# Tying each transfer that sums feed-forward weights to one split of a piece of weights

## The chip, the cores and the metric

The kernel runs on one core of one Trainium2 chip. The metric is the device time of one execution, in microseconds (us): a median of 2010.33 us over three runs, which lay between 2003.17 and 2014.34 us. TensorE (PE) multiplies, VectorE (DVE) and ScalarE (ACT) do the work on elements, GpSimd (POOL) does little arithmetic here, SyncE (SP) only issues transfers. The transfers of all issuers run on the core's 16 DMA engines.

## The reference

Two blocks of a language model work on one sequence of 512 tokens with 1024 features, in float32. The first block projects its normed input on 4104 columns, runs a gated delta rule (4 heads) and a differential attention (4 heads), and projects back. The second block puts 16 tokens in front (528 tokens), and then has a feed-forward layer (`ffn1`), a mixer (retention, and an attention that picks 128 keys for each query), a second feed-forward layer (`ffn2`) and a norm. Its core, cut down:

```python
def swiglu(u, w_gate, w_up, w_down):                     # w_gate, w_up: 1024 x 2816
    return (jax.nn.silu(u @ w_gate) * (u @ w_up)) @ w_down

x = first_block(x, norm_gain, w_in, conv_w, ...)         # gated delta rule, differential attention
h = concatenate([meta, x])                               # 528 tokens
h = h + 0.5 * swiglu(rmsnorm_2(h, ffn1_norm), ffn1_w_gate, ffn1_w_up, ffn1_w_down)
h = h + hybrid_mixer(rmsnorm_2(h, mix_norm), ...)
h = h + 0.5 * swiglu(rmsnorm_2(h, ffn2_norm), ffn2_w_gate, ffn2_w_up, ffn2_w_down)
y = rmsnorm_2(h, final_norm)[:, 16:]
```

## The kernel before

**Stages.** The program runs `block1`, `ffn` for ffn1, `mixer` and `final` (which holds ffn2). Features lie on the 128 partitions, tokens along the rows. Every product is made of float32r parts: weights and activations are split in a high and a low part, and three matmuls (lines 302 to 304, or 1042) make one product.

**The stream of weights.** All weights pass through one list of jobs. `_dma` (line 184) issues a load on SP's queue, into one of two buffers `wraw` (up to 512 KB) or one of eight buffers `fraw` (256 KB, quarters of feed-forward weights). `_conv` (line 249) then splits a piece of at most four 128x128 tiles: ACT copies the high part (`_split`, line 237), DVE subtracts it for the low part (line 238). This is the split of a piece of weights; most jobs have two pieces, a quarter has one. `convert` runs up to five pieces (`CONVB`) ahead of the matmuls.

**The sums of weights.** A feed-forward layer computes the gate and the up projection of 19 of its 22 column tiles by a scheme with fewer products, which needs four sums of weight quarters for each tile. `sum_weights` (line 206) makes them in DRAM: 80 transfers on POOL's queue for each layer (line 227), plain copies and copies that add to what lies there (`accum_op`), into ten tiles `wsums` (named `wsffn...` in the profile). The ten tiles are worked off in groups of three: 24 transfers for each of three groups, and 8 for the last tile. `sum_weights` is a generator: `_conv` asks it for the next transfer at every second split in block1, at every third split in ffn1 and in the mixer (lines 261 and 262, `bgn`). So this sets where a transfer stands in the program. It does not set when it starts: a transfer waits only for earlier transfers on the same tile, and for its turn on POOL's queue. The feed-forward stage reads the sums back as `fraw` quarters; such a load waits for the transfers that it depends on.

**What else stands in block1.** The projections (line 909 and after) run on PE in program order. Beside them a chain of small steps works on the gated delta rule: gates, a row vector sent through DRAM and loaded to all partitions (`rd`, line 562: four loads of 1 MB into `slot`), for each of four heads the decay matrix (DVE line 579, a triangular select on POOL line 580, ACT line 582, DVE lines 591 to 602), an inverse (lines 616 to 700) whose blocks go through DRAM (`db`, line 610; `dx`, lines 624 and 626), and a scan. Another chain works on the differential attention, and sends a norm through DRAM once for each head (`rdfd`, line 785, `krow`, line 788, used on DVE at line 791 and then on PE at line 819). A scheduler sets the order on each engine from the program and its own estimate of times.

Of the kernel before, what the change touches and what calls it, by code (L numbers as in the profile page):

```python
# [12 lines left out]
AF = mybir.ActivationFunctionType  # L13
OP = mybir.AluOpType
AX = mybir.AxisListType

D = 1024
KB = 8
# [150 lines left out]
class Net:  # L169
# [36 lines left out]
    def sum_weights(self, n):  # L206


        nc, a = self.nc, self.a
        nf = 22 - PLAIN  # L210
        out = self.wsums[n] = [self.dram.tile([min(2, nf - i), 4, 128, 4, 128], F32, name=f"ws{n}{i}")
                               for i in range(0, nf, 2)]
        rows = lambda x: x.rearrange("n p k c -> p n k c")

        def src(i, x):
            f = PLAIN + 2 * i
            o = 4 if x in "GU" else 0
            return a[n + ("_gate" if x in "gG" else "_up")][f:f + out[i].shape[0], :, o:o + 4, :]

        steps = (((0, "u"), (2, "g")), ((0, "U"), (2, "u")), ((1, 0),), ((1, "g"),), ((3, 1),), ((3, "G"),))  # L220
        for i0 in range(0, len(out), 3):
            for j, step in enumerate(steps):
                for i in range(i0, min(i0 + 3, len(out))):
                    for d, x in step:
                        y = out[i][:, x] if isinstance(x, int) else src(i, x)
                        kw = {"accum_op": OP.add} if j in (1, 3, 5) else {}
                        nc.gpsimd.dma_start(rows(out[i][:, d]), rows(y), **kw)
                        yield

    def _split(self, j, x):  # L230

        n, ncol = x.shape[1:]
        if j < len(self.joblist) - self.kept:
            hi, lo = (self.wpool.tile([128, n, ncol], F32R, name=y, tag=y, bufs=self.CONVB) for y in ("whi", "wlo"))
        else:
            hi, lo = self.keep(n)
        self.nc.scalar.copy(hi, x)  # L237
        self.nc.vector.tensor_sub(lo, x, hi.bitcast(F32))  # L238
        return hi, lo

# [8 lines left out]
    def _conv(self):  # L249

        j, k = self.j_conv, self.k_conv
        raw = self.raws[j]
        nk = raw.shape[1]
        n = min(self.CK, nk - k)
        hi, lo = self._split(j, raw[:, k:k + n, :])
        his, los = self.convd.setdefault(j, ([], []))
        his += [hi[:, i, :] for i in range(n)]
        los += [lo[:, i, :] for i in range(n)]
        self.n_conv += 1
        self.k_conv += n  # L260
        if self.n_conv % self.bgn == 0:
            next(self.bg, None)
        if self.k_conv == nk:
            self.raws.pop(j)
            if self.joblist[j][0] == "f":
                self.f_done += 1
            else:
                self.p_done += 1
            self.j_conv, self.k_conv = j + 1, 0
            self.prefetch()  # L270
# [124 lines left out]
    def block1(self):  # L395
# [3 lines left out]
        with es:  # L399
# [8 lines left out]
            def params():  # L408
# [4 lines left out]
                V.tensor_mul(lamv[:, 0::2, :], lamv[:, 0::2, :], lamv[:, 1::2, :])  # L413
                V.reduce_sum(lam, lamv[:, 0::2, :], axis=AX.X)
                A.activation(lam, lam, AF.Exp)
# [1296 lines left out]
```

## Time and profile before

| | |
|---|---|
| median of three runs | 2010.33 us |
| profiled execution | 2014.84 us, its span 2013.0 us |
| PE busy | 1920.7 us (95% of the span) |
| DVE busy | 1284.2 us (64%) |
| ACT busy | 904.4 us (45%) |
| POOL busy | 153.6 us (8%) |
| moved by DMA | 281.36 MB |
| POOL's queue (q0) | 79.70 MB, 17.4% of the 16 engines' span |
| SP's queue (q1) | 198.60 MB, 30.6% |

The stages lie in the span about so: block1 from 0 to 452 us, ffn1 to 800 us (its two stretches of quarters at 482 to 563 and 628 to 739 us), the mixer to about 1640 us, then ffn2 and the end. In a table by stretches, PE's busy time against the length of the stretch tells where PE stood still; the granted clock tells in which of its two levels (1.0 is 2.4 GHz, 0.5 is 1.2 GHz) it ran; the DMA share is the busy share of the 16 engines. Line numbers in the rows are those of the kernel before. In the changed kernel the same lines stand one to three lines further down.

### The profile page before, as it was taken

How to read it: one execution, taken by the hardware profiler on the slowest of the kernel's cores; microseconds unless marked ns; L12 is line 12 of the kernel's file. 1: busy time of each engine (PE TensorE's matmuls, PEld its weight loads, DVE VectorE, ACT ScalarE, POOL GpSimd, SP SyncE). 2: the span in 40 equal slices, each digit the busy share in tenths (PEclk: the TensorE clock that was granted, in tenths of full speed). 3: DMA queues.
4: the chain of work that ended last, by engine and by line, in shares of the span. 5: the costliest groups of instructions: out<-in, count | busy, mean ns of one | idle time of the engine just before them, and what ended most of it. 6: DMA issues, size and time to landing. Idle time of an engine off the chain costs nothing.

```text
span 2013.0 us, 31731 instructions
## 1 busy us (share of the span) xinstructions
PE 1920.7 (95%) x12138; PEld 1705.7 (85%) x12138; DVE 1284.2 (64%) x2590; ACT 904.4 (45%) x1774; POOL 153.6 (8%) x179
## 2 busy tenths in 40 slices
PE   6957878999999999999999999999999999999998
PEld 3746657889999999888989898888888889989997
DVE  3645654766746765889755454687764467756764
ACT  3523444555634653445343434344443346634653
POOL 3322432320000000000000000000000000000000
PEclk8978878999999999999999999999999999999999
DMA  9999999994534533321222221211122234535532
GB/s 278 264 245 229 256 240 234 268 249 139 181 105 143 182 110 97 114 73 69 95 68 95 69 89 61 97 63 64 64 74 95 94 122 138 185 108 156 183 103 92
DMA packets 119607, 281.36 MB, mean 140 GB/s; under 512 B 16192, under 2 KB 18720, under 8 KB 119392
## 3 DMA queue, kind: packets, MB, share of 16 engines
q1 hardware_dynamic: 86816, 198.60, 30.6%
q0 software_dynamic: 31552, 79.70, 17.4%
q8 instruction: 95, 1.56, 0.3%
q10 hardware_dynamic: 1088, 1.05, 0.1%
q14 instruction: 56, 0.46, 0.1%
HBM read 276.63 MB, written 82.36 MB: 178 GB/s over the span
## 4 chain that ended last, share of the span: by engine, by line
PE 82%; DMA 12%; DVE 3%; issue 2%; POOL 0%; ACT 0%; SPq 0%; DVEq 0%; POOLq 0%; ACTq 0%
PE pm L302 18%; PE pm L304 18%; PE pm L303 18%; PE pm L1042 11%; DMA wsffn<-in_ffn_up 4%; PE so L1042 3%; PE sc L1042 3%; PE st L1042 3%; DMA wsffn<-wsffn 2%; DMA wsffn<-in_ffn_gate 2%; PE sc L302 2%; PE sc L303 1%; PE sc L304 1%; DMA krow<-rdfd 1%; DVE rot L1208 1%
## 5 line engine op out<-in xcount | busy, mean ns | idle before, releaser
L237 ACT CAST whi<-wraw 128x512 fp32r<-128x512 f32 (+1 forms) x476 | 276.9, 584 | 611.9 <-PE pm L303 462.1
L302 PE MATMUL pm<-xhi,whi 128*128 128x264 f32 (+3 forms) x1448 | 503.7, 348 | 12.0 <-DVE xc L909 10.9
L303 PE MATMUL pm<-xlo,whi 128*128 128x264 f32 (+3 forms) x1448 | 495.8, 342 | 0.0
L304 PE MATMUL pm<-xhi,wlo 128*128 128x264 f32 (+3 forms) x1448 | 494.5, 341 | 0.0
L238 DVE TENSOR_TENSOR wlo<-wraw,whi 128x512 fp32r<-128x512 f32 (+1 forms) x476 | 305.1, 641 | 220.5 <-ACT whi L237 211.3
L302 PEld LDWEIGHTS pm<-xhi,whi 128*128 128x128 f32 (+1 forms) x1448 | 276.4, 191 | 46.7 <-DVE xc L909 11.3
L304 PEld LDWEIGHTS pm<-xhi,wlo 128*128 128x128 f32 (+1 forms) x1448 | 276.1, 191 | 31.3 <-issue 2.7
L303 PEld LDWEIGHTS pm<-xlo,whi 128*128 128x128 f32 (+1 forms) x1448 | 276.4, 191 | 28.6 <-issue 2.0
L237 ACT CAST whi<-fraw 128x512 fp32r<-128x512 f32 x266 | 164.8, 619 | 155.0 <-PE pm L1042 30.3
L238 DVE TENSOR_TENSOR wlo<-fraw,whi 128x512 fp32r<-128x512 f32 x266 | 183.4, 690 | 72.0 <-ACT whi L237 53.7
L302 PE MATMUL pm<-ahi,whi 128*128 128x264 f32 (+1 forms) x506 | 160.1, 316 | 0.0
L304 PE MATMUL pm<-ahi,wlo 128*128 128x264 f32 (+1 forms) x506 | 159.9, 316 | 0.0
L303 PE MATMUL pm<-alo,whi 128*128 128x264 f32 (+1 forms) x506 | 159.3, 315 | 0.0
L1042 PE MATMUL pm<-thi,whi 128*128 128x264 f32 (+1 forms) x456 | 129.7, 284 | 0.0
L1042 PE MATMUL pm<-thi,wlo 128*128 128x264 f32 (+1 forms) x456 | 129.1, 283 | 0.0
L1042 PE MATMUL pm<-tlo,whi 128*128 128x264 f32 (+1 forms) x456 | 129.0, 283 | 0.0
L302 PEld LDWEIGHTS pm<-ahi,whi 128*128 128x128 f32 x506 | 95.2, 188 | 6.0
L303 PEld LDWEIGHTS pm<-alo,whi 128*128 128x128 f32 x506 | 95.2, 188 | 5.9
L304 PEld LDWEIGHTS pm<-ahi,wlo 128*128 128x128 f32 x506 | 95.1, 188 | 5.9
L1632 POOL TENSOR_TENSOR hg<-hg,rcol 128x256 f32<-128x256 f32 x4 | 2.8, 730 | 1198.8 <-ACT rcol L1627 1198.8
L1042 PEld LDWEIGHTS pm<-thi,whi 128*128 128x128 f32 x456 | 86.6, 190 | 0.9 <-DVE u L1082 0.9
L1042 PEld LDWEIGHTS pm<-tlo,whi 128*128 128x128 f32 x456 | 86.7, 190 | 0.0
(482 smaller groups left out, 3842.3 us busy)
## 6 DMA issues: line engine op xcount, KB each, us to landing
wraw<-in_w_in SPq DMA_DIRECT2D x124, 512.0 KB, 3.3
fraw<-wsffn SPq DMA_DIRECT2D x152, 256.0 KB, 2.7
wsffn<-in_ffn_up POOLq DMA_DIRECT2D x54, 512.0 KB, 15.7
wsffn<-in_ffn_gate POOLq DMA_DIRECT2D x54, 512.0 KB, 10.8
fraw<-in_ffn_gate SPq DMA_DIRECT2D x76, 256.0 KB, 2.8
wsffn<-wsffn POOLq DMA_DIRECT2D x36, 512.0 KB, 8.2
wraw<-in_ffn_down SPq DMA_DIRECT2D x32, 384.0 KB, 3.0
wraw<-in_ffn_down SPq DMA_DIRECT2D x32, 320.0 KB, 2.8
```

The costliest lines, as they stand in the source:

```text
L237: self.nc.scalar.copy(hi, x)
L238: self.nc.vector.tensor_sub(lo, x, hi.bitcast(F32))
L302: mm(ps, whi, xhi, start=start, stop=False, **kw)
L303: mm(ps, whi, xlo, start=False, stop=False, **kw)
L304: mm(ps, wlo, xhi, start=False, stop=stop, **kw)
L1042: ins = P.matmul(p, y[k], x(k)[z], start=first and k == i == 0, stop=last and k == 3 and i == 2, skip_group_check=True)
L1208: V.tensor_mul(tmp[o:o + half], p[i:i + half], tab[i:i + half, 1, t:T])
L1632: nc.gpsimd.tensor_mul(o, o, rc)
```

## The change

`sum_weights` now yields first, before any transfer, and then gives each transfer's instruction to its caller. `_split` keeps the instruction of ACT's copy. `_conv` leaves the first eight splits without a transfer, and from the tenth on makes each transfer wait for the split at which it stands. All 160 transfers get such a wait, plain ones and adding ones.

```diff
+AFTER = mybir.DependencyInfo(mybir.DependencyClass.Sync, mybir.DependencyReason.DATA)
...
         rows = lambda x: x.rearrange("n p k c -> p n k c")
+        yield
...
-                        nc.gpsimd.dma_start(rows(out[i][:, d]), rows(y), **kw)
-                        yield
+                        yield nc.gpsimd.dma_start(rows(out[i][:, d]), rows(y), **kw)
...
-        self.nc.scalar.copy(hi, x)
+        self.split_ins = self.nc.scalar.copy(hi, x)
...
-        if self.n_conv % self.bgn == 0:
-            next(self.bg, None)
+        if self.n_conv > 8 and self.n_conv % self.bgn == 0:
+            ins = next(self.bg, None)
+            if ins is not None:
+                self.tc.add_manual_dep(ins.ins, self.split_ins.ins.name, AFTER, reason="spread over the stage")
```

On POOL's queue, before, the first triangular select of block1 (line 580) and the memset of line 627 stand behind 51 transfers. `wsffn_100` to `wsffn_102` are the tiles of the third group of ffn1; `DMASW` is the semaphore of an earlier transfer.

```order
L227 DMA wsffn_100<-in_ffn_gate 128x2x512
L227 DMA wsffn_101<-in_ffn_up 128x2x512
L580 AFFINE_SELECT te<-te 128x512 [waits DVE_49]
L227 DMA wsffn_101<-in_ffn_gate 128x2x512
...
L227 DMA wsffn_100<-in_ffn_up 128x2x512 [waits DMASW6_49,DMASW0_49]
L580 AFFINE_SELECT te<-te 128x512 [waits DVE_49]
L227 DMA wsffn_100<-in_ffn_up 128x2x512 [waits DMASW7_49,DMASW1_49]
```

The same place now. `wsffn_95` and `wsffn_96` belong to the first group; `Activation` is the semaphore of ACT's split.

```order
L229 DMA wsffn_95<-in_ffn_up 128x2x512 [waits DMASW3_49,Activation_49]
...
L583 AFFINE_SELECT te<-te 128x512 [waits DVE_49]
L229 DMA wsffn_96<-in_ffn_up 128x2x512 [waits DMASW4_49,Activation_49]
...
L583 AFFINE_SELECT te<-te 128x512 [waits DVE_49]
L229 DMA wsffn_94<-wsffn_94 128x2x512 [waits DMASW6_49,Activation_49]
L583 AFFINE_SELECT te<-te 128x512 [waits DVE_49,Pool_49]
L229 DMA wsffn_95<-wsffn_95 128x2x512 [waits DMASW0_49,Activation_49]
L229 DMA wsffn_96<-wsffn_96 128x2x512 [waits DMASW2_49,Activation_49]
L583 AFFINE_SELECT te<-te 128x512 [waits DVE_49,Pool_49]
```

Ten transfers stand ahead of the first select instead of 51, and 15 ahead of the fourth. Each has a wait for ACT beside its waits for earlier transfers.

On PE the scheduler moved 62 of 11626 instructions, all inside block1. One such place is the inverse, where PE waits for the blocks that come back from DRAM (`slot`, line 637). Before:

```order
L302 MATMUL pm<-xhi,whi 128x512
L637 MATMUL pd<-slot_127,slot_125 32x32
L303 MATMUL pm<-xlo,whi 128x512
...
L819 MATMUL pf<-dfk,dfq 128x512
L302 MATMUL pm<-xhi,whi 128x512
L303 MATMUL pm<-xlo,whi 128x512
L637 MATMUL pd<-slot_127,slot_125 32x32 x31
```

and now:

```order
L822 MATMUL pf<-dfk,dfq 128x512
L640 MATMUL pd<-slot_126,slot_124 32x32
L305 MATMUL pm<-xhi,whi 128x512
...
L307 MATMUL pm<-xhi,wlo 128x512
L640 MATMUL pd<-slot_126,slot_124 32x32 x31
L784 MATMUL pt<-cst,rdf 8x128
```

The first of the 32 small products stands behind two products of the attention instead of ahead of them, and the other 31 stand behind twelve further matmuls of a projection. No matmul is added or dropped. ACT gets two more loads of an activation table, in block1.

## Rows read from the trace of the kernel before

**Rows 1.** Stretches: length, busy us (instructions) of PE, PEld, DVE, ACT, POOL; clock, DMA share, GB/s.

```profile
0.00:48.00 48.00, 30.28 (x82) 15.76 (x83) 17.02 (x39) 18.61 (x32) 15.22 (x21) 0.89 0.99 285
120.00:204.00 84.00, 50.06 (x220) 40.72 (x219) 37.51 (x83) 18.44 (x27) 25.89 (x29) 0.76 0.98 234
204.00:304.00 100.00, 81.93 (x397) 58.85 (x396) 59.25 (x218) 45.40 (x108) 38.89 (x45) 0.81 1.03 250
304.00:406.00 102.00, 92.61 (x690) 77.92 (x689) 60.35 (x132) 52.72 (x133) 34.72 (x36) 0.95 0.99 247
0.00:452.00 452.00, 369.68 (x1955) 288.94 (x1956) 255.56 (x619) 196.16 (x394) 149.17 (x169) 0.88 1.00 251
482.00:563.00 81.00, 81.00 (x672) 81.00 (x670) 62.48 (x110) 49.46 (x96) 0.00 (x0) 1.00 0.58 177
628.00:739.00 111.00, 111.00 (x919) 111.00 (x919) 86.77 (x153) 67.65 (x130) 0.00 (x0) 1.00 0.53 161
739.00:1640.00 901.00, 899.02 (x5377) 792.08 (x5377) 586.67 (x1181) 366.80 (x729) 0.24 (x4) 1.00 0.24 82
```

**Rows 2.** POOL in order of time: start, duration, the last transfer that it issues.

```profile
457.44 0.81 POOL L227 DMA_DIRECT2D wsffn<-in_ffn_gate  x1 [4.48 <-DMA wsffn<-wsffn]
```

**Rows 3.** Transfers of 0 to 452 us: queues, then issues with median us to landing.

```profile
q0 software_dynamic: 31376, 79.18, 77.1%
q1 hardware_dynamic: 16369, 33.92, 22.7%
...
wraw<-in_w_in SPq DMA_DIRECT2D x32, 512.0 KB, 7.5
slot<-rd SPq DMA_DIRECT2D x4, 1024.0 KB, 17.5
```

**Rows 4.** Issues of 482 to 2013 us, with median us to landing.

```profile
wraw<-in_w_in SPq DMA_DIRECT2D x92, 512.0 KB, 3.3
...
dec<-in_decay SPq DMA_DIRECT2D x4, 264.0 KB, 2.8
...
diag<-in_dfmask SPq DMA_DIRECT2D x1, 64.0 KB, 2.7
```

**Rows 5.** PE's waits of 0 to 452 us: total, times, longest us.

```profile
PE pf L819 <- DVE dfk L791: 16.1, 4, 7.7
PE pm L302 <- DVE xc L909: 10.9, 1, 10.9
PE pd L302 <- ACT xhi L356: 10.7, 5, 7.5
PE pt L523 <- ACT td L512: 9.9, 1, 9.9
PE pd L589 <- DVE slot L600: 8.3, 1, 8.3
PE pd L637 <- DMA slot<-dx: 7.8, 1, 7.8
```

**Rows 6.** Waits of all engines, 0 to 460 us.

```profile
ACT whi L237 <- DMA wraw<-in_w_in: 72.3, 9, 27.8
...
DVE te L579 <- DMA slot<-rd: 28.6, 3, 14.4
...
ACT xhi L356 <- DMA hT<-in_hT: 10.6, 7, 2.3
...
ACT te L582 <- POOL te L580: 4.5, 1, 4.5
```

**Rows 7.** ACT's waits of 0 to 48 us.

```profile
ACT whi L237 <- DMA wraw<-in_w_in: 8.9, 4, 3.8
```

**Rows 8.** PE in the eleven stretches near half clock: their sum.

```profile
sum 76.00, PE 67.92; mean PE 6.17
```

**Rows 9.** Chain that ended last, 300 to 340 us: start, duration.

```profile
312.67 6.92 DMA rdfd<-rTf
...
320.11 7.93 DMA krow<-rdfd
```

## The prediction

> **What bounds the kernel now.** I read the table by stretches first, then POOL's queue, then PE's waits. In the table the reader is to compare PE's busy time with the length of each stretch. From 482 us on they are equal within a quarter of a per cent in the rows shown, at full clock: the feed-forward layer and the mixer run at PE's pace [rows 1]. From 0 to 452 us PE is busy 369.68 us, so it stands still for 82.3 us, at a mean granted clock of 0.88 [rows 1]. All that this change can win lies there. The idle time is not spread evenly: 17.7 us fall in 0 to 48 us, 33.9 in 120 to 204, 18.1 in 204 to 304, 9.4 in 304 to 406, and the small rest between.
>
> The same row gives the reason that I take: the 16 DMA engines are busy 1.00 of the time there, against 0.24 to 0.58 later [rows 1]. POOL's queue takes 77.1% of it and SP's, which feeds the projections, 22.7% [rows 3]. POOL has issued its last transfer at 457 us [rows 2], and no later stretch shows any of its 160. So the sums of both feed-forward layers, whose places in the program reach to the end of the mixer, all run ahead into block1, since nothing on POOL's queue holds them. What they cost is seen in the landings: a load of 512 KB takes 7.5 us in block1 and 3.3 later [rows 3, 4]; the 1 MB loads of the row vectors take 17.5 us [rows 3]. ACT waits 72.3 us for pieces of weights, with one wait of 27.8, and DVE 28.6 us for the row vectors [rows 6]. PE's own longest waits name DVE and ACT, but those stood behind a transfer.
>
> **What the change does to the transfers.** Counting in the code: block1 has 41 jobs of two pieces, and `convert` runs up to five pieces ahead, so the rule of every second split, from the tenth to the 84th, places 38 transfers in block1. The other 42 of ffn1 follow at every third split, 87 to 210: 3 ahead of the first stretch of quarters, 19 in it (pieces 95 to 150), 11 in the products behind it, 9 in the first 28 pieces of the second stretch. The 80 of ffn2 need 240 pieces, and the mixer has about 250, so they end in time. Block1 then carries 38 transfers where it carried 160. One transfer's price is 0.771 x 452 = 348 us of all 16 engines for 79.18 MB [rows 1, 3], so 2.3 us for 512 KB. 38 of them are 87 us; SP's own load is 0.227 x 452 = 103 us; together about half of a block1 of 380 us. The transfers then come near to landing as they do after 482 us.
>
> **The sum**, against the profiled execution (2014.84 us, of which 2013.0 are the span).
>
> 1. Opening, 0 to 48 us. ACT waits 10.6 us for the input blocks [rows 6] and 8.9 for weights [rows 7]. Blocks of 264 KB land in 2.8 us when the engines are free [rows 4]. PE's wait for the first high parts is 10.7 us [rows 5]. Of 17.7 us idle I leave 6, because the first load still has to land and ACT still works on eight blocks one by one: 12 us, and 2 more for the stretch at half clock that follows. 14 us.
> 2. Row vectors, 120 to 204 us: 33.9 us idle, of which 10.9, 9.9 and 8.3 are the three large waits [rows 5]. All hang on `slot<-rd`. Scaled as the 512 KB load (3.3 to 7.5), 17.5 us become 7.7. Some 10 us less for each of the three loads that DVE waits for would cover 28.6 us of waiting [rows 6]; as a shorter load can still be late, I set 25 us won and 9 left.
> 3. Round trips through DRAM, 204 to 406 us: 27.5 us idle. The last one for the attention takes 6.92 out and 7.93 back [rows 9]; with a small transfer at 2.7 us [rows 4] the pair is 5.4, so this trip gets 9.4 us shorter, more than PE's longest wait for one (7.7). PE waits 16.1 us in four such trips and 7.8 for the inverse, 23.9 together [rows 5]; the earlier trips have less to lose: 20 us.
> 4. Clock. PE works 67.9 us in eleven stretches near half clock, the first at 40 to 48 us, the last at 328 to 335 [rows 8]; they lie at and behind its idle times. At full clock this work would take at best half, 34 us less. Some of it is counted in term 1, a quarter of the stalls remains, and short matmuls (a column or two) don't gain: 18 us.
> 5. Waits added in block1. POOL's queue is in order, and the four selects now stand behind transfers that wait for a split (10 transfers ahead of the first, 15 ahead of the fourth). Behind a late select are ACT's exponential, DVE's products for that head, and PE's next pair of products for the chain. The split that is waited for is at most five pieces ahead of PE, and the scheduler put the selects after splits that its order finishes earlier. I take 0; the far end is 4.5 us for each of four selects, the row in which ACT waits for a select stuck behind transfers today [rows 6], 18 us.
> 6. The transfers in ffn1. In 482 to 563 us SP uses 0.58 x 81 = 47 us of the engines [rows 1], and 19 transfers at 2.3 us add 44: 91 us of work in 81. Eight raw buffers, and five split pieces, lie between a late load and PE, and the transfers themselves may lag: the last sum of a group stands 14 pieces or more ahead of the issue of the load that reads it. So between 0 and 10 us here, and 0 to 4 in the second stretch (0.53 share). I take 5 in all.
> 7. The transfers in the mixer: 80 x 2.3 = 184 us over 901, so a share of 0.24 becomes 0.44. The feed-forward stretches run at 0.58 with PE never idle [rows 1]; 0, at most 10.
> 8. Two table loads on ACT, some 2 us of 452 in which ACT is busy 196 [rows 1]: 0, at most 3.
>
> Sum: 14 + 25 + 20 + 18 - 5 = 72 us faster. 2014.84 - 72 = 1943, and as the median lies 4.5 us below the profiled execution, 1938 us.
>
> At term 6 a rule speaks against the change. The rows show SP's queue with 22.7% beside POOL's 77.1 [rows 3], but SP had not always something to move, so they don't show who yields. The Trainium skill (DMA: Bandwidth & Descriptors, in Queues, rings and completion order) says that each DMA engine takes turns between the queues that have work, a packet at a time. By that rule, POOL's queue could hold half of every engine while it has a backlog, and SP, which wants 0.58, would not come first. No run here shows it yet; its mechanism and time are the first rival.
>
> **Rivals.**
> - *Half shares in ffn1.* While POOL's queue has a backlog, SP gets 0.5 of the engines where it wants 0.58 and 0.53 [rows 1]. The first stretch grows by 0.58/0.5, 13 us, the third of the second one in which transfers stand by 2 us or more; with the slower loads of the down products I set 18 in place of 5. 1951 us. For it: 91 us of work in 81. Against: each transfer is held to a split, so a backlog is short. Chance 0.12.
> - *The chains were late anyway.* DVE is busy 59 to 60% in 204 to 406 us, and the chains are serial; with the transfers quick, PE waits for the same steps of DVE and ACT. Then terms 2 to 4 give half, 31 us in place of 63, and the sum is 40: 1970 us. For it: PE's waits name DVE in most rows [rows 5]. Against: those rows have a transfer behind them [rows 6]. Chance 0.14.
> - *Every transfer stalls PE where PE was full.* 122 transfers move to stretches with no slack on PE. If each makes a load of weights late by more than the buffers cover, PE loses up to the whole 2.3 us. It decides at 77/122 = 0.63 us each: above that the kernel is slower than before. At 0.8 us it is 98 us lost against 77 won, 2031 us. Against it: even with the engines full, PE stood still for only 9.4 us in 304 to 406 us. Chance 0.05.
> - *The waits hold nothing.* If the splits they name were long done when POOL comes to a transfer, all would run ahead as now: no change, 2010 us. Splits can't run more than five pieces ahead of the matmuls, which speaks against it. Chance 0.04.
>
> **How the numbers follow.** My forecast, 1938 us, has the other 0.65. Its own range takes the unknown ends: at best 82.3 idle less 6, plus 34 of clock, no loss in ffn1, so 110 faster, 1900 us; at worst terms 1 to 4 at half (38), 14 lost in ffn1, so 24 faster, 1986 us. These ends are unlikely together; I give 1903 to 1978, which holds the first two rivals too and leaves out the last two and the tails. A measurement of this kernel can tell about 0.5% (10 us) from no change. Faster by more than that: 0.65 + 0.12 + 0.14, less 0.01 for the worst ends, 0.90. Within: 0.05. Slower: 0.05.
>
> **What would show it.** In the changed profile POOL's transfers spread to about 1600 us, the DMA share in block1 falls to about a half, `wraw` lands in 3 to 4 us and the 1 MB loads in 6 to 9. Block1 ends near 375 us with some 20 us idle on PE and a clock above 0.95. The first stretch of quarters takes 81 to 91 us with a share near 1; the mixer keeps its 901 us. Wrong would be: PE idle in block1 above 50 us although the share has fallen (the chains), waits of PE or ACT on `fraw` of more than 10 us in ffn1, waits on `wraw` in the mixer, or POOL's select late by several us behind a transfer.

## The result, and the profile after

The changed kernel takes 1927.16 us (median of four runs, 1917.47 to 1936.44), against 2011.74 us for the kernel before; the ratio is 0.9586, with a 95% interval of 0.9519 to 0.9654. The forecast was 1938 us, so the kernel came out 11 us faster than forecast. The profiled execution took 1936.44 us, 78.4 us less than the profiled one of before. Its four runs lie in two pairs, at 1917 to 1920 us with a mean granted clock of 0.994 and at 1935 to 1936 us with one of 0.985, and the profile shows one of the second pair.

First the table by stretches of the changed kernel, with the columns of [rows 1]:

```profile
0.00:48.00 48.00, 42.10 (x190) 30.02 (x191) 33.02 (x72) 34.28 (x57) 3.22 (x8) 1.00 0.58 194
120.00:204.00 84.00, 79.26 (x407) 61.33 (x405) 66.56 (x224) 42.40 (x92) 12.99 (x14) 0.96 0.57 153
204.00:304.00 100.00, 99.71 (x794) 82.43 (x794) 69.24 (x167) 64.51 (x160) 7.65 (x9) 1.00 0.38 109
304.00:372.00 68.00, 67.12 (x398) 59.64 (x397) 46.38 (x79) 39.14 (x64) 10.12 (x10) 1.00 0.74 193
0.00:372.00 372.00, 352.89 (x2106) 287.18 (x2107) 268.75 (x645) 212.69 (x418) 44.89 (x52) 0.98 0.57 155
387.00:462.00 75.00, 75.00 (x622) 75.00 (x621) 57.96 (x103) 46.30 (x89) 15.90 (x17) 1.00 0.98 288
482.00:563.00 81.00, 81.00 (x672) 81.00 (x671) 45.60 (x80) 31.94 (x63) 13.61 (x16) 1.00 0.82 217
765.00:807.00 42.00, 42.00 (x129) 29.85 (x130) 22.58 (x50) 11.95 (x24) 1.26 (x2) 0.51 0.25 54
807.00:1540.00 733.00, 732.26 (x4276) 642.21 (x4275) 470.52 (x970) 295.25 (x594) 64.75 (x71) 1.00 0.47 127
```

The reader is to see three things. Block1 runs at a DMA share of 0.57 where it had 1.00, and PE stands still for 19.1 us of 372. The first quarters run from 387 us at a share of 0.98, with PE busy all of the time. And the mixer has 42 us at half clock (0.51) in which PE is busy throughout; before, the mean clock of its stretch was 1.00 [rows 1].

Where the time went follows from three marks on PE and POOL: the first quarter of ffn1 starts on PE at 387.0 us (before 485.2), the mixer's first memset on POOL at 709.62 (before 806.92), the last quarter of ffn2 at 1862.8 (before 1941.6). So block1 gave 98.2 us, ffn1 cost 0.9 (322.6 in place of 321.7), and the stretch from the mixer on cost 18.5 (1153.2 in place of 1134.7).

POOL's transfers, the last of ffn1 and the first of ffn2, against [rows 2]:

```profile
567.04 0.81 POOL L229 DMA_DIRECT2D wsffn<-in_ffn_gate  x1 [3.92 <-ACT c L1077]
...
711.45 0.76 POOL L229 DMA_DIRECT2D wsffn<-in_ffn_up  x1 [1.59 <-ACT whi L238]
```

Each now waits for a split (behind a group of them the row names what ACT did just before), and the 160th is issued at 1544 us. Queues and landings of 0 to 372 us, against [rows 3]:

```profile
q1 hardware_dynamic: 17152, 35.99, 29.0%
q0 software_dynamic: 8330, 21.26, 27.4%
...
wraw<-in_w_in SPq DMA_DIRECT2D x32, 512.0 KB, 5.2
...
slot<-rd SPq DMA_DIRECT2D x4, 1024.0 KB, 12.5
```

The waits of all engines in the same stretch, against [rows 5, 6]:

```profile
POOL wsffn L229 <- ACT whi L238: 293.2, 39, 23.7
...
ACT whi L238 <- DMA wraw<-in_w_in: 16.6, 5, 7.8
...
ACT te L585 <- POOL te L583: 11.8, 3, 5.5
...
PE pd L305 <- ACT xhi L359: 5.2, 1, 5.2
...
DVE te L582 <- DMA slot<-rd: 5.1, 1, 5.1
...
PE pf L822 <- DVE dfk L794: 4.4, 2, 3.6
...
PE pt L526 <- ACT td L515: 3.7, 1, 3.7
```

ACT waits 16.6 us for weights where it waited 72.3, DVE 5.1 for the row vectors where it waited 28.6, and no wait of PE is longer than 5.2 us. POOL waits 293.2 us for splits: that is the change itself. In block1 the rows show one engine that pays for it, ACT, which waits 11.8 us for selects.

The 42 us at half clock begin at the mixer's opening, in order of time:

```profile
755.25 0.69 POOL L229 DMA_DIRECT2D wsffn<-in_ffn_gate  x1 [9.95 <-ACT whi L238]
...
762.50 1.14 ACT L238 CAST whi<-wraw 128x512 fp32r<-128x512 f32 x2 [5.33 <-DMA wraw<-in_w_in]
763.54 0.51 ACT L1201 CAST ih<-yr 128x384 fp32r<-128x384 f32 x1
...
763.95 0.37 ACT L1244 ACTIVATE yr<-sc 128x256 f32<-128x256 f32 x1
...
764.38 0.38 PE L305 MATMUL sc<-ih 64*128 64x256 f32 x1 [2.52 <-ACT yr L1244]
...
765.97 0.42 PE L307 MATMUL pm<-xhi,wlo 128*128 128x264 f32 x1
```

ACT takes its instructions in the order shown. It waits 5.33 us for a load of weights, the two splits and a cast stand ahead of the activation of the index scores (line 1244), and PE waits 2.52 us for that. From there on PE works at half clock until 807 us. In the kernel before the same place had waits of 3.68 us on ACT and 0.81 us on PE (at 860 us), and no half clock. Some 41 us at half clock are some 20 us lost, about what lies between the two pairs of runs.

### The profile page after: what moved, and what is told of

The parts are those of the page before. It is cut to its first block, busy times and chain, and to the rows that moved or that the text cites. A ratio compares the mean times of both kernels' runs of the same rounds, so it can differ in the third digit from the quotient of the medians.

```text
span 1934.4 us, 31826 instructions
## 1 busy us (share of the span) xinstructions
PE 1903.0 (98%) x12138; PEld 1697.7 (88%) x12138; DVE 1284.6 (66%) x2590; ACT 906.9 (47%) x1776; POOL 154.5 (8%) x179
## 4 chain that ended last, share of the span: by engine, by line
PE 92%; DVE 3%; DMA 3%; ACT 1%; issue 1%; SPq 0%; DVEq 0%; ACTq 0%
PE pm L305 20%; PE pm L307 20%; PE pm L306 20%; PE pm L1045 11%; PE so L1045 3%; PE sc L1045 3%; PE st L1045 3%; PE sc L305 2%; PE sc L306 1%; PE sc L307 1%; DVE rot L1211 1%; PE pf L822 1%; DMA wraw<-in_w_in 1%; DMA slot<-rd 1%; DMA wraw<-in_ffn_down 1%
## 5 line engine op out<-in xcount | busy, mean ns | idle before, releaser
L229 POOL DMA_DIRECT2D wsffn<-in_ffn_up x60 | 58.5, 976 | 487.0 <-ACT whi L238 448.9
L229 POOL DMA_DIRECT2D wsffn<-in_ffn_gate x60 | 58.4, 974 | 452.5 <-ACT whi L238 392.5
```

What stands on the lines that cost most here:

```text
L229: yield nc.gpsimd.dma_start(rows(out[i][:, d]), rows(y), **kw)
```

## Experiments

All ratios are to the kernel before, with 95% intervals. "First quarter" is the first mark above.

**Which of the waits matter.** Only ffn1's 80 transfers wait:

```diff
-            if ins is not None:
+            if ins is not None and "ffn2" not in self.wsums:
```

> Only the 80 transfers of ffn1 wait for their splits; those of ffn2 have no wait, but stand behind them on POOL's queue. PE and DVE keep, instruction for instruction, the order of the kernel before. Theory (the load on the DMA engines in block1 is what cost the time): block1 is as short as with all waits, first product of the quarters at 385 to 395 us (before 485.2, changed kernel 387.0), although nothing is moved on PE and DVE. Rival (the moved instructions made the gain): it begins at 470 to 485. From about 567 us on the 80 transfers of ffn2 run without a pause beside the second stretch of quarters. If queues take half shares there, that stretch grows from 111 us to 113 to 120; if each transfer stalls PE, by 20 us or more. Total 1920 to 1945 us by the theory, about 2005 by the rival of the order.

Measured: 2005.59 us, 0.9957 [0.9934, 0.998]; first quarter 479.4. My expectation was wrong, and the rival's numbers came out. But the order on POOL's queue shows that the load was not taken away:

```order
L229 DMA wsffn_7927<-in_ffn_up 128x2x512
L229 DMA wsffn_7927<-in_ffn_gate 128x2x512
...
L229 DMA wsffn_7928<-wsffn_7928 128x2x512
L229 DMA wsffn_94<-in_ffn_up 128x2x512
L229 DMA wsffn_7929<-wsffn_7929 128x2x512
```

These are the first transfers on the queue; tiles 7927 and up are ffn2's, and tile 94 is ffn1's, behind fourteen of them. The scheduler put transfers that wait for nothing ahead of those that do, so the load in block1 stayed, and the run does not decide for the rival:

```profile
120.00:204.00 84.00, 45.91 (x207) 37.57 (x207) 37.47 (x83) 18.82 (x27) 26.82 (x31) 0.78 1.00 241
204.00:304.00 100.00, 74.93 (x321) 52.77 (x321) 57.55 (x213) 43.86 (x105) 26.79 (x30) 0.81 0.91 217
...
500.00:600.00 100.00, 99.56 (x819) 99.15 (x819) 62.77 (x114) 45.65 (x90) 18.54 (x21) 1.00 0.89 252
```

So waits on half of the transfers, with the load in place, gain almost nothing. The last line: ffn1 at a share of 0.89 lost 0.44 us in 100.

The other half, only ffn2's transfers wait:

```diff
+            if ins is not None and "ffn2" in self.wsums:
```

> Only the 80 transfers of ffn2 wait; those of ffn1 run ahead from the tenth split's place as before, in the first 200 to 240 us. Order on PE and DVE as in the kernel before. Theory: the stalls of the opening and of the row vectors (to 204 us) stay, the round trips behind about 230 us get short. First product of the quarters at 440 to 465 us, total 1960 to 1990 us. Rival (any wait on POOL's queue or the late start made the gain): close to the changed kernel, 1917 to 1936.

Measured: 1991.89 us, 0.9881 [0.9845, 0.9917]; first quarter 450.0, as expected, the total a little above the range.

```profile
120.00:204.00 84.00, 50.53 (x227) 40.70 (x225) 38.43 (x86) 19.19 (x28) 26.93 (x31) 0.78 1.01 243
204.00:304.00 100.00, 92.04 (x688) 70.28 (x687) 70.78 (x245) 58.30 (x132) 11.21 (x14) 0.95 0.48 124
```

With the order of PE's and DVE's instructions that the kernel before has, the stall of 120 to 204 us stays as it was [rows 1] while the engines are full, and 204 to 304 us recovers 10 us of PE as soon as the share falls to 0.48. The order is unchanged, so this gain is the load's. The profiled execution also had a wait of 1.9 us on the index scores and half clock behind it (0.63 from 815 to 870 us), some 20 us that I had not counted in the total.

All 160 transfers wait, but only for the tenth split:

```diff
+            if self.n_conv == 10:
+                self.split10 = self.split_ins
...
-                self.tc.add_manual_dep(ins.ins, self.split_ins.ins.name, ...)
+                self.tc.add_manual_dep(ins.ins, self.split10.ins.name, ...)
```

> All 160 transfers wait for the tenth split alone, so they start late (about 24 us) and then run ahead as before. Order on PE and DVE as in the kernel before. Theory (load in block1): the opening gains 10 to 18 us, the rest of block1 stays as before; first product of the quarters at 465 to 478 us, total 1990 to 2003 us. Rival (the late start was the main thing): 1930 to 1945 us.

Measured: 2016.13 us, 1.0013 [0.9988, 1.0038], a miss; first quarter 485.6.

```profile
0.00:48.00 48.00, 40.46 (x182) 28.67 (x183) 32.46 (x71) 33.03 (x55) 12.19 (x17) 1.00 0.81 243
...
204.00:304.00 100.00, 70.51 (x387) 51.19 (x387) 50.08 (x175) 37.28 (x90) 34.55 (x40) 0.74 1.01 250
```

The opening got its 10 us (40.46 for 30.28 [rows 1]), and the same load, pushed later, took them back from the chains: PE has 11.4 us less in 204 to 304 us than before. Here, sparing the opening was worth nothing by itself.

**How much there is to win.** No transfer at all. The quarters that would read sums read as many bytes of plain weights, so this kernel leaves out the sums and computes something else:

```diff
-            ins = next(self.bg, None)
+            ins = None
```

> Leaves out all 160 transfers; the quarters that would read the sums read plain weights instead, as many bytes. Theory: this is the floor that freeing the DMA engines can reach. First product of the quarters at 370 to 387 us, ffn1 and the mixer without any loss, total 1895 to 1918 us. Rival (the chains are late anyway and hold what is left): block1 within 4 us of the changed kernel, 383 to 391.

Measured: 1904.35 us (1902.93 to 1905.53), 0.9447 [0.9403, 0.949]; first quarter 376.3, no half clock in the mixer. Both numbers are in the ranges of the theory. Of the 107 us between this kernel and the one before, the change takes some 85.

The changed kernel again, with three others on one chip:

> The changed kernel once more, beside the next ones on the same chip. Executions fall in two groups, about 1918 and 1935 us; the profile shows which one it is by the clock behind PE's wait in the index scores, at about 764 us: 40 us at half clock when PE waited 2 us or more there (the longer group), full clock when it waited about 1 us or less.

Measured: 1924.43 us (1915.84 to 1939.05), 0.9563 [0.9527, 0.9599]; the profiled run of 1937.97 has the wait on the index scores again, 3.1 us, and 0.55 clock from 760 to 805 us. Of the ten runs of this kernel four took 1934 us or more, at clocks of 0.983 to 0.985, and one lies between, at 1928 us and 0.989.

No transfer of ffn2 before the index scores stand in the program:

```diff
+            self.bgn = 2                      # behind the index scores
...
-    net.bg = net.sum_weights("ffn2")
+    net.bg, net.bgn = net.sum_weights("ffn2"), 10 ** 9
```

> No transfer of ffn2 before the index scores of the mixer are emitted; then one at every second split. Theory (transfers beside the weights of the index make ACT late, PE waits some 2.5 us, and the clock stays at half for 40 us behind it): the wait goes back to about 0.8 us, no half clock in the mixer, all executions near 1917, spread under 8 us. Rival (the two groups come from the chip and not from transfers): two groups as before, median 1920 to 1936.

Measured: 1922.53 us, 0.9557 [0.953, 0.9583]. Five runs at 1919 to 1928, but the profiled one at 1938.78, with two waits on the index scores (2.3 us together) and a clock of 0.56 from 770 to 805 us. So the theory missed in that run. But the place in the program did not keep the transfers out of the index scores:

```profile
762.89 0.76 POOL L229 DMA_DIRECT2D wsffn<-in_ffn_up  x1 [51.90 <-ACT whi L238]
...
771.45 0.44 PE L305 MATMUL sc<-ih 64*128 64x384 f32 x1 [1.49 <-ACT yr L1244]
```

The first wait, 0.84 us, ends at 763.86, when this transfer has only just been issued. The longer one, 1.49 us, ends 8.6 us after the issue, and the half clock begins there. So this kernel does not show the half clock without a transfer beside it.

Block1 with a transfer at every split (75 of them):

```diff
-    net.bg, net.bgn = net.sum_weights("ffn1"), 2
+    net.bg, net.bgn = net.sum_weights("ffn1"), 1
```

> The waits as in the change, but one transfer at every split of block1 instead of every second: 75 transfers in block1 in place of 38, every one tied to its split. Theory (load in block1): by a straight line between 38 transfers (first product of the quarters at 387.0) and 160 (485.2), 417; as an engine share of about 0.7 leaves room, 395 to 417 us; total 1930 to 1960. Rival (the wait itself, or the order that goes with it, made the gain, whatever the load): 385 to 390, total 1917 to 1936.

Measured: 1948.82 us, 0.9667 [0.9634, 0.9699]; first quarter 404.5, as expected. The profiled execution has a wait of 1.8 us on the index scores, and a clock of 0.54 from 780 to 825 us.

**Where in block1 they cost.** Two kernels hold back ffn2's transfers as above, leave splits 25 to 38 of block1 (the row vectors) without a transfer, and put transfers elsewhere; the first at splits 51 to 66:

```diff
-        if self.n_conv > 8 and self.n_conv % self.bgn == 0:
+        n = self.n_conv
+        every = 1 if 50 < n <= 66 else self.bgn
+        if n > 8 and n % every == 0 and not 24 < n <= 38:
```

> As the one that spares the index, and in block1 no transfer at the splits 25 to 38 (where the 1 MB row vectors are loaded), one at every split from 51 to 66 instead. Theory (what is left of the loss in block1 lies at the row vectors): first product of the quarters at 379 to 384 us (387.0 with the change, 376.3 without any transfer), total 1906 to 1914. Rival (the floor is not reached because of the share as a whole): 386 to 390.

Measured: 1922.14 us (1918.79 to 1925.65), 0.9537 [0.9521, 0.9553]; first quarter 393.3, a miss. The row vectors cost less (from 100 to 110 us PE is busy 8.60 us, in the changed kernel 4.39), but a new stall stands in the inverse.

The second puts them at splits 67 to 82, in the output projection, where nothing on PE waits for a round trip:

```diff
+        every = 1 if 66 < n <= 82 else self.bgn
```

> As the experiment that left out the transfers at splits 25 to 38, but these now stand at every split from 67 to 82, in the output projection of block1, where PE has no chain beside it (before, they stood at 51 to 66, beside the inverse's round trip). 40 transfers in block1. No transfer of ffn2 before the index scores. Theory: a transfer in block1 costs where a serial chain through DRAM runs, and nothing where PE is bound by its own matmuls; so 378 to 384 us to the first quarter, and 1905 to 1918 in all. Rival: only the number of transfers in block1 counts; 387 plus or minus 2, and 1917 to 1925. A third: sixteen transfers one behind the other with the engines full make the weights of the output projection late: above 390.

Measured: 1908.14 us (1907.5 to 1910.62), 0.9484 [0.9471, 0.9497]; first quarter 372.8, below the expectation, and below the 376.3 of the kernel without any transfer, which is thus no floor. The order of the instructions on PE, DVE and ACT is the same in these two kernels and in the one without transfers. The transfers of 187 to 215 us, first where they stand at every split from 51:

```profile
q0 software_dynamic: 972, 2.38, 43.5%
...
dx<-slot SPq DMA_DIRECT2D x1, 256.0 KB, 8.1
slot<-dx SPq DMA_DIRECT2D x4, 64.0 KB, 4.0
```

and where they stand at every second split there:

```profile
q0 software_dynamic: 500, 1.22, 22.4%
...
dx<-slot SPq DMA_DIRECT2D x1, 256.0 KB, 4.7
slot<-dx SPq DMA_DIRECT2D x4, 64.0 KB, 2.1
```

The pair takes 12.1 us in the one and 6.8 in the other. PE's wait for it is 4.7 us in the first, with a clock of 0.79 from 200 to 240 us, and is absent in the second, where the clock is 1.00. POOL has issued 44 transfers before the first quarter in each of the two, so the 20.5 us between them (393.3 and 372.8) go with the place alone. The second is 16 to 19 us faster than the changed kernel, which has 43, but there the order of the instructions differs too.

**How much ffn1 takes.** Fewer transfers in block1 (every third split) and more in ffn1 (every second; the mixer has that rate too), with the order of the kernel without transfers:

```diff
-    net.bg, net.bgn = net.sum_weights("ffn1"), 2
+    net.bg, net.bgn = net.sum_weights("ffn1"), 3
...
-    net.bgn = 3
+    net.bgn = 2
```

> The changed kernel, but with a transfer at every third split in block1 (25 or 26 transfers in place of 38) and at every second split in ffn1 (in place of every third). It asks two things. First the curve of block1: its ends so far are 376.3 us to the first quarter with no transfer, 387.0 with 38, 404.5 with 75, 485.2 with 160, which bends; so 380 to 385 here. Second, what ffn1 does with more load than it has in the changed kernel, where 387 to 462 us already show a DMA share of 0.98 with PE busy 75.00 of 75. My theory: the loads of quarters have eight raw buffers and five split pieces of cover, and a transfer that lags costs nothing, so ffn1 (first quarter to the mixer's first memset, 322.5 us in the changed kernel) takes 322 to 326, and the total is 1910 to 1922 where the mixer doesn't fall to half clock, up to 1940 where it does. Rival, half shares: loads and transfers together now want more than the engines have for some 110 us, POOL's queue has a backlog there, and SP's loads get half where they want 0.58: PE waits for quarters, ffn1 takes 335 us or more, and the kernel is no faster than the changed one (1925 to 1945). A third: a sum arrives after the load that reads it was due; then a single wait of several us stands at the start of a group.

Measured: 1938.22 us, 0.9653 [0.9627, 0.9678]; first quarter 377.6, below my 380 to 385, but ffn1 took 337.5 us: the rival was right here.

```profile
380.00:460.00 80.00, 75.38 (x609) 73.95 (x608) 54.80 (x99) 44.18 (x87) 23.32 (x25) 1.00 1.07 308
460.00:540.00 80.00, 73.29 (x583) 72.57 (x583) 33.09 (x62) 20.00 (x41) 15.65 (x18) 0.96 0.84 217
```

The queues of the changed kernel, 387 to 462 us:

```profile
q0 software_dynamic: 3365, 8.68, 49.8%
q1 hardware_dynamic: 7032, 12.82, 48.0%
```

and of this one, 380 to 460 us:

```profile
q0 software_dynamic: 4913, 12.46, 63.6%
q1 hardware_dynamic: 6655, 12.12, 42.8%
```

and of the kernel before, 482 to 563 us:

```profile
q1 hardware_dynamic: 7762, 14.26, 57.0%
```

In the kernel before 177 GB/s moved in the quarters, nearly all of it SP's [rows 1]. In the changed one SP's queue moves 12.82 MB in 75 us, 171 GB/s, short by 0.5 MB. Here it moves 12.12 in 80, 152 GB/s, short by 2.0 MB, and eight raw buffers of 256 KB hold 2 MB. That would explain why PE loses nothing in the first and 4.6 us in these 80 us; it is worked out, and the number of buffers was not varied.

It does not explain the rest of the 15 us. PE's longest wait in ffn1 stands behind the quarters, at the first product with the down weights:

```profile
475.64 0.62 ACT L238 CAST whi<-wraw 128x512 fp32r<-128x512 f32 x1 [12.55 <-DMA wraw<-in_ffn_down]
...
476.84 0.59 PE L305 MATMUL pm<-ahi,whi 128*128 128x264 f32 x1 [5.88 <-ACT ahi L1029]
```

ACT's cast of the activations (line 1029) stands behind a split for whose weights ACT waits 12.55 us; they come through the two `wraw` buffers. In the changed kernel ACT waits 6.60 us at this place, and no wait of PE in ffn1 is longer than 0.4 us. About 6.8 us at half clock go with PE's wait (0.50 from 475.0 to 481.8 us).

Both at once, with ffn2's transfers held back as above: eight transfers at splits 10 to 24, none at 25 to 66, one at every split from 67, and every second split in ffn1:

```diff
+        every = 1 if 66 < n <= 86 else self.bgn
+        if n > 8 and n % every == 0 and not 24 < n <= 66:
...
-    net.bgn = 3
+    net.bgn = 2
```

> Both at once: in block1 eight transfers at splits 10 to 24, none at 25 to 66, one at every split from 67 on (28 in all); in ffn1 at every second split; no transfer of ffn2 before the index scores. Theory: block1 takes what it takes without any transfer (376.3 us) plus what the first eight cost, 377 to 381; ffn1 322 to 326; in all 1902 to 1914, faster than the changed kernel by 5 us or more. Rivals: ffn1 overloaded, 335 us and more and no gain; or the first group's sums, which now come last in block1, are late for the loads that read them, with one wait of 3 us or more on PE at the first quarters.

Measured: 1925.76 us, 0.9567 [0.9552, 0.9582]; first quarter 373.9, below the 377 to 381 expected, but ffn1 335.4 us: the total missed, and the rival of an overloaded ffn1 was right. Block1 gains nothing beyond what the better placing gave (372.8), and ffn1 loses 12 us against that kernel's 323.7.

The first quarter against the number of transfers that block1 carries by the code, at even spacing but for the last column:

```
transfers in block1     0      26      38      75      160
first quarter, us     376.3   377.6   387.0   404.5   485.2
```

One more costs 0.05 us each up to 26, 0.8 up to 38, 0.5 up to 75, 1.0 beyond. These are not prices of the load alone: only the first two columns have the same order on PE, DVE and ACT, each of the others has another.

## Why the prediction was right, and where its terms were off

The main reading holds: the load of 160 transfers in block1 held the chains up, and taking it away gives block1 back. With the order of before and half of the load gone, 35 us come back; with that order, the load in place and waits added, 6 us and none; with no load, 109 (485.2 less 376.3).

*Idle time (terms 1 to 3).* Forecast 12 of the opening's idle time, 25 and 20, 57 us together. Measured from the stretches: the opening 17.7 to 5.9, so 11.8; the row vectors 33.9 to 4.7, so 29.2; the rest of block1 27.5 to 1.2, so 26.3. Against that the 48 to 120 us stretch went from 2.3 us idle to 7.3, because the row vectors' stall now lies partly there (100 to 110 us): net 63.2. The `slot<-rd` load takes 12.5 us, not the 7.7 that I scaled, and `wraw` 5.2, not 3 to 4, and the round trip's waits on PE fell to 4.4 us.

*Clock (term 4): the term that was mis-sized.* Forecast 18, and 2 in term 1. From the marks, PE was busy 485.2 - 82.3 = 402.9 us to the first quarter before, and 387.0 - 19.1 = 367.9 after: 35.0 us. Most of it is the clock. PE's stretches at half clock up to the first quarter, before and after:

```profile
sum 105.70, PE 71.04; mean PE 6.46
...
sum 13.60, PE 11.99; mean PE 4.00
```

Work at half clock fell from 71.0 to 12.0 us, and half of the difference is 29.5. The other 5.5 us of busy time are not explained. [Rows 8] had it: 67.9 us near half clock, half of it 34. I cut this for what was counted elsewhere, for stalls that remain, and for short matmuls. But terms 1 to 3 counted idle time only, and a stretch at half clock is busy time, so hardly anything was counted twice; and the stalls that remained left little half clock. 63.2 + 35.0 are the 98.2 us.

*Selects (term 5).* They are late, as the far end had it: ACT waits 11.8 us in three waits, up to 5.5, where it waited 4.5 once. PE shows none of it. 0 was right.

*ffn1 (term 6).* 0.9 us for the 5 taken. The rival of half shares had the shares right and the price wrong at this load: POOL's queue does hold 49.8% of the engines and SP's 48.0% where it used 57.0, and PE lost nothing in these 75 us. One step more load, and ffn1 costs 13 to 15 us more, more than half of it behind the first quarters. The Trainium skill (DMA: Bandwidth & Descriptors, in Queues, rings and completion order) lets each engine take turns between queues with work, a packet at a time. The changed kernel's shares would fit that, but no row shows whether SP's queue had work waiting there; the 63.6 against 42.8 of the heavier one show POOL's queue with more than half.

*Mixer (term 7): wrong in four of ten runs, perhaps five.* I took 0, at most 10, because the feed-forward stretches are never idle at a higher share. The profiled execution lost 18.5. The step that failed is that the cover of one stage was taken for that of another: the mixer loads weights through two buffers, and behind ACT's split of a late one stand the index scores. The wait itself is small; the half clock behind it is the price. In all five profiled executions with 31 to 41 us of it (the changed kernel twice, only ffn2's transfers held, one transfer at every split, and ffn2's held back) POOL had issued a transfer 8 to 10 us before PE's wait ended. In the four profiled kernels without any transfer in the mixer the wait was 0.4 to 1.1 us, with no half clock. That speaks for the transfers, but does not settle it: the three kernels that also placed block1's transfers anew had transfers beside the index scores, a wait of 0.4 us and no half clock, and no execution of the changed kernel near 1918 us was profiled.

*The other rivals.* That the chains were late anyway falls: PE waits 4.4 us in round trips where it waited 16.1. That every transfer stalls PE falls: the 122 moved transfers cost 0.9 us in ffn1 and 18.5 behind it, 0.16 us each. That the waits hold nothing falls with POOL's 293 us of waiting.

In sum: 21 us more from block1 than forecast, 4 less lost in ffn1, 18.5 lost in the mixer in the profiled run. The forecast for that run, 1942.8, was 6.4 us above it because these errors partly cancel; that the total came so close is luck in part.

The load is shown to cost at a fixed order twice: with the order of before, where half of it is worth 35 us, and in the order that the kernel without transfers shares with the last four experiments, where the first quarter is 376.3 us with no transfer and 393.3 or 372.8 with 44, by their place. Not separated: how much of the changed kernel's own 98.2 us its moved instructions give, since no run has its order with the load of before.

## What to carry to other kernels

A background transfer is not free because its queue is idle: price it at the place where it runs (here it was cheap beside matmuls with deep buffers, dear beside a chain that goes through DRAM), and spread or move it accordingly; waits on only some of the transfers can just let the others run ahead, as in the first experiment. Idle time and half clock are two separate gains, so sum PE's busy time in the stretches at half clock and count half of it, less only what the stalls that stay will keep. The cover of a load is that of its own stage's buffers: price it stage by stage, and look at what else stands behind its split on an engine's queue.

## What the runs showed of the hardware

In four profiled executions of three kernels a wait of PE of 1.8 to 3.1 us on the index scores is followed by about 41 us at half clock, in the changed kernel although PE is busy throughout (42.00 of 42 us at 0.51). Two waits in a fourth kernel, 1.5 us the longer, are followed by about 31 us of it, while single waits of 0.4 to 1.1 us at the same place are followed by none. One kernel with two waits there, 1.6 us the longer, fell only to 0.91 over 20 us, and a wait of 2.5 us later in its mixer was followed by 0.91 over 20 us too. So a wait of 2.5 us can cost some 20 us or 2, by what PE works on behind it or for another reason; the runs don't tell.

At a summed share of 0.98 of the DMA engines PE lost nothing in 75 us of quarters. At 1.07 (380 to 460 us) it lost 4.6 us of 80, and 6.7 in the 80 us behind them, 5.9 of that in one wait. The quarters read from sums landed in 11.6 us in place of 6.5 (median of 380 to 540 and 387 to 547 us).
